# Head scaling and chunk work behind the convolution, decay rows behind exponentials, a later gate load, rotation in fewer operations

## The chip, the core and the metric

The kernel runs on one core of a Trainium2 chip. The metric is the device time of one execution in microseconds (us); smaller is better. The engines are TensorE (PE), VectorE (DVE), ScalarE (ACT), GpSimd (POOL) and SyncE (SP), which here only issues DMA transfers. Each engine runs its own instructions in the order in which they stand in its queue: an instruction that waits holds up all that stands behind it on that engine.

## What is computed

Two layers of a backbone over 512 latent tokens and 256 context tokens, in float32. Each layer normalises, projects once, and splits into three groups: a neighbourhood attention, a two-directional state-space mixer and a grouped-query attention. The lines that this change touches compute the following.

```
q = rms_norm(q.reshape(b, n, GQA_Q_HEADS, HEAD_DIM), q_norm_w)
k = rms_norm(k.reshape(b, n, GQA_KV_HEADS, HEAD_DIM), k_norm_w)
...
q = axial_rope(q, rows, cols)            # xh * cos + concat(-x2, x1) * sin
k = axial_rope(k, rows, cols)
...
xbc = jax.nn.silu(depthwise_conv(xbc, conv_w, conv_b))
...
seg = a_cum[:, :, :, None, :] - a_cum[:, :, None, :, :]
decay = jnp.exp(jnp.where(causal, seg, -jnp.inf))
g = jnp.einsum('bcthn,bcshn->bctsh', cr, br) * decay
y_diag = jnp.einsum('bctsh,bcshp->bcthp', g, xr)
...
y = y.reshape(zz.shape).astype(zz.dtype) * jax.nn.silu(zz)
```

Behind the mixers stand an output projection and a gated feed-forward block. The second layer (the last) gives results for the 512 latent tokens only.

## The kernel before

Float32 products on TensorE are made of pairs of a high and a low part, three matmuls each. A layer runs in stages. First come the projections of queries, keys and values; among them `p_kv` and `p_q`, which for each tile of 128 tokens take the raw grouped-query heads (one array of keys and two of queries, called here heads 0, 1 and 2) into `raws` (tile GR) and collect their sums of squares.

Then a loop runs over eight convolution blocks b. `p_xbc(b)` projects 128 channels over all tokens on TensorE (L348, into the PSUM tile S), VectorE clears the gap between context and latent tokens (memset L766), ScalarE takes the middle tap (L768), VectorE adds four taps (L773, four operations), ScalarE makes the tanh (L778) and VectorE finishes (L780, L782); one block later `p_xtr` transposes the result on TensorE (L796, six transposes in two halves), and ScalarE copies it out (L802). In the first layer, tiles of the gate z are projected between the blocks (L362), evacuated by ScalarE and VectorE (L814, L815) and written to DRAM (zsp). The loop also calls, for b below 3, `head_out(b)`: POOL multiplies the raw head by its norm weight, tile by tile (L680), and by the cosine (L686); VectorE makes the product with the sine in eight strided operations (L696, the rotation), adds (L697), and scales by the inverse root of the mean square (L699 for latent tokens, L701 for context tokens). `head_tr(b - 1)` transposes the head one block later (L708) and writes it to DRAM (gq). POOL meanwhile works through products for the next stage's modulation vectors (L239, 128x512 each), whose sums ScalarE takes (L240), and one power (L280) for the inverse roots of all heads, followed by the VectorE operations L282, L283 and L285.

Then 48 attention units (32 in the second layer) follow. Each makes scores on TensorE (L400, L403), a maximum on VectorE, the exponential on ScalarE (L420), the normalisation on POOL (L425), transposes (L434), their copies on ScalarE (L438) or VectorE (L440), and the product with the values (L446). Between units the list of events `ev` feeds in other work: `tick` advances the chunk work `diag` of the mixer by a step (two decay tiles wh and wl loaded from DRAM, crow, by SP; ScalarE's four decay-row additions L913; VectorE's L917, four; ScalarE's exponential L919; products on VectorE L924 to L933 and on POOL L928; matmuls L938 and L939), `steps` carries the chunk states, and `load_z`, the event at unit 6, has SP load z back into HZ (L1017).

What decides the order on each engine is a scheduler, which places the instructions by times that it simulates itself. `tc.issue_after(x)` is a constraint on it: what is traced in its block may not be placed ahead of instruction x on x's engine. It adds no wait, and it binds only the instructions of that one engine. The stages before the heads, the output projection and the feed-forward blocks are not touched by the change.

## Time and profile before

| | us |
|---|---|
| median of 3 runs | 1830.81 (1829.63 to 1834.84) |
| profiled execution | 1828.21 |
| its span | 1826.4 |
| TensorE busy | 1733.7 (95%) |
| VectorE, ScalarE, POOL busy | 1066.0, 682.7, 399.6 |
| mean granted TensorE clock | 0.976 |

The profiled execution lies 2.6 us under the median. In the 40 slices of the page the convolution blocks and the attention of the first layer lie at 150 to 450 us, those of the second at 1140 to 1400 us. A busy share is an average over stages: what a change to one stage is worth is read from the waits in that stage.

### The profile page before, as it was taken

To read this page: it belongs to the slowest core of one execution; us is meant where nothing else is said; L and a number is where in the kernel's file an instruction comes from. 1 tells how busy PE (TensorE), PEld (TensorE's weight loads), DVE (VectorE), ACT (ScalarE), POOL (GpSimd) and SP (SyncE) were. 2 spreads that over 40 slices of the span, in tenths; PEclk is the share of its full clock that TensorE was granted. 3 is DMA by queue.
4 is the path that set the end of the run, shared out by engine and by line. 5 is a ranking of instruction groups with operands and counts; after the bars stand their busy time and mean duration, and the time that the engine had idled before them with its cause. 6 is when DMAs were issued, how large, how long until landed. Compare 5 with 4: busy or idle time off the path is not lost.

```text
span 1826.4 us, 26611 instructions
## 1 busy us (share of the span) xinstructions
PE 1733.7 (95%) x10146; PEld 1475.2 (81%) x10146; DVE 1066.0 (58%) x2165; ACT 682.7 (37%) x1376; POOL 399.6 (22%) x429
## 2 busy tenths in 40 slices
PE   7998897899999999999999989998899999999998
PEld 3887785777878888888888878987777888888887
DVE  4659776886575455445554575576686743333334
ACT  4655664556253211121122234334555532222222
POOL 0398875643020000000000010421552100000000
PEclk9999998999989999999999999999899999999999
DMA  9643655422224343333344455233522333333332
GB/s 363 218 145 112 203 153 150 121 87 67 64 70 127 116 126 108 123 103 109 124 118 120 124 159 186 82 115 110 151 72 65 99 93 92 104 93 94 102 106 79
DMA packets 94319, 221.66 MB, mean 121 GB/s; under 512 B 18416, under 2 KB 26224, under 8 KB 94192
## 3 DMA queue, kind: packets, MB, share of 16 engines
q1 hardware_dynamic: 78096, 204.65, 36.6%
q10 hardware_dynamic: 16096, 15.31, 2.5%
q8 instruction: 80, 1.31, 0.3%
q14 instruction: 47, 0.39, 0.1%
HBM read 198.49 MB, written 21.43 MB: 120 GB/s over the span
## 4 chain that ended last, share of the span: by engine, by line
PE 77%; DVE 9%; DMA 6%; ACT 4%; issue 2%; POOL 2%; SPq 0%; ACTq 0%; DVEq 0%; POOLq 0%
PE S L348 60%; PE sm L446 3%; DMA wl<-crow 2%; PE PT L434 2%; PE PT L348 1%; PE PT L362 1%; PE sm L362 1%; DMA wr<-in_mod_wT_dram 1%; PE S L400 1%; PE sm L938 1%; PE sm L939 1%; PE PT L983 1%; DVE MB L773 1%; PE PT L996 1%; DVE wl L337 1%
## 5 line engine op out<-in xcount | busy, mean ns | idle before, releaser
L336 ACT ACTIVATE wh<-wr 128x1024 fp32r<-128x1024 f32 (+2 forms) x204 | 198.0, 972 | 723.8 <-PE S L348 550.7
L337 DVE TENSOR_TENSOR wl<-wr,wh 128x1024 fp32r<-128x1024 f32 (+2 forms) x204 | 231.2, 1134 | 178.9 <-ACT wh L336 177.0
L280 POOL TENSOR_TENSOR tiny<-tiny,mhalf 128x2 f32<-128x2 f32 (+2 forms) x17 | 28.7, 1689 | 1066.4 <-DVE tiny L1195 1018.7
L348 PE MATMUL S<-HY,wh 128*128 128x512 f32 (+1 forms) x716 | 215.8, 359 | 5.6 <-ACT HY L329 4.0
L348 PE MATMUL S<-HZ,wh 128*128 128x512 f32 (+1 forms) x716 | 213.4, 356 | 1.0 <-DVE HZ L330 1.0
L348 PE MATMUL S<-HS,wh 128*128 128x512 f32 (+1 forms) x716 | 213.0, 355 | 0.0
L348 PE MATMUL S<-HY,wl 128*128 128x512 f32 (+1 forms) x716 | 212.8, 355 | 0.1
L348 PE MATMUL S<-HS,wl 128*128 128x512 f32 (+1 forms) x716 | 209.7, 351 | 0.0
L242 DVE CUSTOM_DVE_ANT_0 PT<-wr,XFB 128x512 f32<-128x512 f32 x112 | 75.6, 716 | 185.6 <-DMA wr<-in_mod_wT_dram 185.5
L348 PEld LDWEIGHTS S<-HY,wh 128*128 128x128 f32 x716 | 118.6, 191 | 24.5 <-ACT HY L329 4.2
L348 PEld LDWEIGHTS S<-HZ,wh 128*128 128x128 f32 x716 | 119.5, 192 | 23.0 <-DVE HZ L330 2.8
L348 PEld LDWEIGHTS S<-HY,wl 128*128 128x128 f32 x716 | 118.8, 192 | 19.5 <-DVE wl L337 0.4
L348 PEld LDWEIGHTS S<-HS,wh 128*128 128x128 f32 x716 | 117.9, 190 | 18.2
L348 PEld LDWEIGHTS S<-HS,wl 128*128 128x128 f32 x716 | 116.6, 189 | 19.0
L348 PE MATMUL S<-PHA,wh 128*128 128x512 f32 (+1 forms) x358 | 105.8, 353 | 0.0
L348 PE MATMUL S<-PHB,wh 128*128 128x512 f32 (+1 forms) x358 | 104.5, 350 | 0.0
L348 PE MATMUL S<-GX,wh 128*128 128x512 f32 (+1 forms) x400 | 97.7, 350 | 0.4 <-DVE KA L1149 0.4
L425 POOL TENSOR_SCALAR pr<-pr,tiny 128x640 f32<-128x640 f32 (+2 forms) x80 | 67.8, 851 | 90.3 <-DVE tiny L424 66.1
L239 POOL TENSOR_TENSOR KA<-QN,XFB 128x512 f32<-128x512 f32 x48 | 68.5, 1430 | 40.8 <-ACT XFB L216 23.1
L434 PE MATMUL PT<-c,pr 128*128 128x128 f32 x384 | 65.0, 286 | 12.8 <-POOL pr L425 5.7
L1296 DVE TENSOR_TENSOR MB<-S,MA 128x768 f32<-128x768 f32 (+1 forms) x42 | 34.6, 823 | 70.7 <-PE S L348 70.7
L348 PEld LDWEIGHTS S<-GX,wh 128*128 128x128 f32 x400 | 65.9, 189 | 11.3 <-DVE KA L1149 0.8
(432 smaller groups left out, 3901.2 us busy)
## 6 DMA issues: line engine op xcount, KB each, us to landing
wr<-in_mod_wT_dram SPq DMA_DIRECT2D x56, 512.0 KB, 3.9
wr<-in_w_gate_dram SPq DMA_DIRECT2D x44, 512.0 KB, 3.6
wr<-in_w_up_dram SPq DMA_DIRECT2D x44, 512.0 KB, 3.6
wr<-in_w_blk_dram SPq DMA_DIRECT2D x28, 512.0 KB, 3.8
wr<-in_w_down_dram SPq DMA_DIRECT2D x32, 448.0 KB, 3.4
QN<-in_mod_wT_dram SPq DMA_DIRECT2D x48, 256.0 KB, 3.0
wr<-in_w_out_dram SPq DMA_DIRECT2D x32, 256.0 KB, 2.7
wr<-in_w_down_dram SPq DMA_DIRECT2D x16, 512.0 KB, 3.5
```

What stands on the lines that cost most here:

```text
L239: G.tensor_tensor(out=p_, in0=wv, in1=x, op=ALU.mult)
L242: V.tensor_tensor_reduce(out=p_, in0=wv, in1=x, scale=1.0, scalar=0.0, op0=ALU.mult, op1=ALU.add, accum_out=acc[:, o : o + 1],)
L280: POW.tensor_tensor(out=y, in0=v, in1=mhalf[:, 0:n], op=ALU.pow)
L336: S.activation(hi, raw, AF.Copy)
L337: V.tensor_tensor(lo, raw, hi.bitcast(F32), ALU.subtract)
L348: ins = PE.matmul(pt[:, c0:c1], lhsT=w, rhs=xx[:, c0:c1], start=(k == (0 if len(order) == 1 else order[0]) and i == 0), stop=(k == (nk - 1 ...
L362: PE.matmul(pt[:, 0:n], lhsT=s, rhs=w[:, o : o + n], start=(k == 0 and i == 0), stop=(k == KB - 1 and i == 2),)
L400: PE.matmul(st[:, o0:512], lhsT=Q[:, q0 : q0 + P], rhs=K[:, xk[0] : xk[1]], start=(i == 0), stop=(i == 1))
L425: G.tensor_scalar(out=p_, in0=p_, scalar1=m[:, 4:5], scalar2=1.0, op0=ALU.mult, op1=ALU.mult)
L434: PE.transpose(pt[:, k * P : (k + 1) * P], pr[j, qi][:, kk * P : (kk + 1) * P], ident)
L446: PE.matmul(pv[64 * j : 64 * j + 64, 0:P], lhsT=V2(kts[k], j), rhs=ph[j, qi][:, k, :], start=(k == 0), stop=(k == nkt - 1), tile_position= ...
L1296: V.tensor_tensor(gg[:, c0:c1], pu[:, c0:c1], sg[:, c0:c1], ALU.mult)
```

## The change

- `head_out(b)` is traced with `issue_after(conv_end[b])`, where conv_end[b] is the last VectorE operation of convolution block b. So VectorE's part of head b stands behind that block's finish. `head_tr` comes one block later (b = 2 to 4 in place of 1 to 3).
- `tick` is traced with `issue_after(conv_end[-1])`: all VectorE operations of the chunk work stand behind the finish of block 7.
- The four decay-row additions are traced with `issue_after(exps[-1])`: on ScalarE they stand behind the exponential that was traced last.
- `load_z` is the event at unit 14, not 6.
- In `head_out`, POOL's six (or four) 128x128 scalings become one of 128x768 (128x512), its four cosine products one of 128x512, and VectorE's eight rotation operations of 128x64 four of 128x128.

```diff
@@ -382,6 +382,8 @@
             r.append(K)
         return r
 
+    exps = []
+
     def attn(V2, xk, kts, qcols, bias, yout):
 
 
@@ -417,7 +419,7 @@
                 V.tensor_reduce(out=m[:, 0:1], in_=st[:, o0:768], op=ALU.max, axis=AX.X)
                 V.tensor_scalar_mul(m[:, 2:3], m[:, 0:1], -1.0)
             p_ = pr[j, qi] = T(sb, "pr", 3, [P, nk])
-            S.activation(p_, st[:, o0:768], AF.Exp, bias=m[:, 2:3], accum_out=m[:, 3:4])
+            exps.append(S.activation(p_, st[:, o0:768], AF.Exp, bias=m[:, 2:3], accum_out=m[:, 3:4]).ins)
 
@@ -674,26 +676,18 @@
             v4 = lambda ap: ap.rearrange("p t (h c) -> p t h c", c=64)
             v7 = lambda ap: ap.rearrange("p t (h f s c) -> p t h f s c", f=2, s=2, c=16)
             nt = n // P
-            for t in range(nt):
-                w3 = wvec.unsqueeze(1).to_broadcast([P, 2, 64])
-                rv = raw[:, t, :].rearrange("p (h c) -> p h c", c=64)
-                G.tensor_tensor(out=rv, in0=rv, in1=w3, op=ALU.mult)
+            w4 = wvec.unsqueeze(1).unsqueeze(1).to_broadcast([P, nt, 2, 64])
+            G.tensor_tensor(out=v4(raw[:, 0:nt, :]), in0=v4(raw[:, 0:nt, :]), in1=w4, op=ALU.mult)
             c = T(sb, "pr", 3, [P, 4, P])
             s = T(sb, "pr", 3, [P, 4, P])
-            for t in range(4):
-                rv = raw[:, t, :]
-                cb = cosT[:, t, :].unsqueeze(1).to_broadcast([P, 2, 64])
-                G.tensor_tensor(
-                    out=c[:, t, :].rearrange("p (h c) -> p h c", c=64), in0=rv.rearrange("p (h c) -> p h c", c=64),
-                    in1=cb, op=ALU.mult,
-                )
+            c4 = cosT.unsqueeze(2).to_broadcast([P, 4, 2, 64])
+            G.tensor_tensor(out=v4(c), in0=v4(raw[:, 0:4, :]), in1=c4, op=ALU.mult)
             sv = sinT.rearrange("p t (f s c) -> p t f s c", f=2, s=2)
-            for h in range(2):
-                x5 = raw[:, 0:4, 64 * h : 64 * h + 64].rearrange("p t (f s c) -> p t f s c", f=2, s=2)
-                o5 = s[:, :, 64 * h : 64 * h + 64].rearrange("p t (f s c) -> p t f s c", f=2, s=2)
-                for f in range(2):
-                    for k in range(2):
-                        V.tensor_tensor(o5[:, :, f, k, :], x5[:, :, f, 1 - k, :], sv[:, :, f, k, :], ALU.mult)
+            x6, o6 = v7(raw[:, 0:4, :]), v7(s)
+            for f in range(2):
+                for k in range(2):
+                    sb4 = sv[:, :, f, k, :].unsqueeze(2).to_broadcast([P, 4, 2, 16])
+                    V.tensor_tensor(o6[:, :, :, f, k, :], x6[:, :, :, f, 1 - k, :], sb4, ALU.mult)
             V.tensor_tensor(c, c, s, ALU.add)
             rb = r[:, 12 * i : 12 * i + 12].rearrange("p (t h) -> p t h", h=2).unsqueeze(3)
             V.tensor_tensor(v4(raw[:, 0:4, :]), v4(c), rb[:, 0:4].to_broadcast([P, 4, 2, 64]), ALU.mult)
@@ -754,6 +748,8 @@
 
         xs = [[slot("GX", F32, (P, 3, 256)) for _ in range(2)] for _ in range(2)]
         Bs, BT, CT, xb = [None] * 2, [None] * 2, [None] * 2, [None] * 8
+
+        conv_end = []
 
         def p_xbc(b):
             conly = last and b >= 6
@@ -777,9 +773,10 @@
             th = pt
             S.activation(th[:, 0:wid], ac[:, 0:wid], AF.Tanh)
             o = ac if b < 4 else slot("GT" if b < 6 else "GC")
-            V.scalar_tensor_tensor(o[:, 0:512], th[:, 0:512], 1.0, ac[:, 0:512], ALU.add, ALU.mult)
+            iv = V.scalar_tensor_tensor(o[:, 0:512], th[:, 0:512], 1.0, ac[:, 0:512], ALU.add, ALU.mult)
             if not conly:
-                V.scalar_tensor_tensor(o[:, 512:768], th[:, 516:772], 1.0, ac[:, 516:772], ALU.add, ALU.mult)
+                iv = V.scalar_tensor_tensor(o[:, 512:768], th[:, 516:772], 1.0, ac[:, 516:772], ALU.add, ALU.mult)
+            conv_end.append(iv.ins)
             if b >= 4:
                 (BT, CT)[b // 6][b % 2] = o
             xb[b] = o
@@ -882,9 +879,10 @@
             if b:
                 p_xtr(b - 1)
             if b < 3:
-                head_out(b, qnw[l] if b else knw[l], r, ntok if b else NT)
-            if 1 <= b < 4:
-                head_tr(b - 1, ntok if b > 1 else NT)
+                with tc.issue_after(conv_end[b]):
+                    head_out(b, qnw[l] if b else knw[l], r, ntok if b else NT)
+            if 2 <= b < 5:
+                head_tr(b - 2, ntok if b > 2 else NT)
 
         def hb(ap, w):
             return ap.unsqueeze(2).to_broadcast([P, ap.shape[1], w])
@@ -908,9 +906,10 @@
                 d_ = nc.sync.dma_start(t.rearrange("p h t -> p (h t)"), crow[i][:, o : o + 512].to_broadcast([P, 512]))
             rows_in.append(d_.ins)
             yield
-            for h in range(4):
-                o = 8 + h0 + h
-                S.activation(Wb[:, h, :], Wb[:, h, :], AF.Identity, bias=ncum[:, c, o : o + 1])
+            with tc.issue_after(exps[-1]):
+                for h in range(4):
+                    o = 8 + h0 + h
+                    S.activation(Wb[:, h, :], Wb[:, h, :], AF.Identity, bias=ncum[:, c, o : o + 1])
             yield
             for h in range(4):
                 o = h0 + h
@@ -1089,6 +1088,10 @@
         st_ = steps()
 
         def tick(t):
+            with tc.issue_after(conv_end[-1]):
+                tick_(t)
+
+        def tick_(t):
             if t % 3 == 1 and t // 3 + 1 < nd:
                 next(dgs[t // 3 + 1])
             for k in range(t // 3, t // 3 - 2, -1):
@@ -1100,7 +1103,7 @@
         ev += [(u, 1, lambda: next(st_, None)) for u in spread_over(36, U[2], U[3])]
         if not last:
             ev.append((U[4], 2, lambda: gate(4, 5)))
-        ev.append((6, 2, load_z))
+        ev.append((14, 2, load_z))
         ev.append((U[5], 2, lambda: gate(1, 2)))
         ev.append((U[6], 2, lambda: gate(0, 3)))
         ev.append((3 * nu / 4, 2, lambda: y_in(1)))
```

How the scheduler's order changes, at three places.

VectorE in the first layer, at the finish of convolution block 0. GR_1206 is head 0, GR_1207 and GR_1208 are heads 1 and 2; MB is the convolution's result and S its PSUM tile; tiny_37x are the inverse roots. Before:

```order
L282 SCALAR_TENSOR_TENSOR tiny_372_1748<-tiny_371_1746 128x36
L283 TENSOR_TENSOR tiny_372_1748<-tiny_372_1748,tiny_370_1744 128x36
L285 SCALAR_TENSOR_TENSOR tiny_373_1751<-tiny_372_1748,tiny_371_1746 128x36
L659 MEMSET tiny_1873_10643 128x36
L699 TENSOR_TENSOR GR_1206<-pr_1853,tiny_373_1751 128x512
L701 TENSOR_TENSOR GR_1206<-GR_1206,tiny_373_1751 128x256
L701 TENSOR_TENSOR GR_1207<-GR_1207,tiny_373_1751 128x256
L701 TENSOR_TENSOR GR_1208<-GR_1208,tiny_373_1751 128x256
L780 SCALAR_TENSOR_TENSOR MB_1809<-S_1759,MB_1809 128x512
L782 SCALAR_TENSOR_TENSOR MB_1809<-S_1759,MB_1809 128x256
L697 TENSOR_TENSOR pr_2009<-pr_2009,pr_2010 128x512
L766 MEMSET S_1876 128x4
```

The same place now:

```order
L282 SCALAR_TENSOR_TENSOR tiny_372_1748<-tiny_371_1746 128x36
L283 TENSOR_TENSOR tiny_372_1748<-tiny_372_1748,tiny_370_1744 128x36
L776 SCALAR_TENSOR_TENSOR MB_1809<-S_1759,MB_1809 128x512
L778 SCALAR_TENSOR_TENSOR MB_1809<-S_1759,MB_1809 128x256
L690 TENSOR_TENSOR pr_1849<-GR_1206,c_214 128x8x16
L285 SCALAR_TENSOR_TENSOR tiny_373_1751<-tiny_372_1748,tiny_371_1746 128x36
L690 TENSOR_TENSOR pr_1849<-GR_1206,c_214 128x8x16 x3
L661 MEMSET tiny_1873_10607 128x36
L695 TENSOR_TENSOR GR_1206<-GR_1206,tiny_373_1751 128x256
L691 TENSOR_TENSOR pr_1848<-pr_1848,pr_1849 128x512
L693 TENSOR_TENSOR GR_1206<-pr_1848,tiny_373_1751 128x512
L762 MEMSET S_1864 128x4
```

The finish of the block (L780 and L782, now L776 and L778) has moved ahead of the head's scalings; the rotation of head 0 (now L690), which stood in the stage before, has moved in between it and the memset of block 1 (L766, now L762).

VectorE in the first layer, convolution block 5; zt is the gate's tile. Before:

```order
L766 MEMSET S_2517 128x4
L815 SCALAR_TENSOR_TENSOR zt_2602<-zt_2602,sm_2577 128x256
L773 SCALAR_TENSOR_TENSOR MB_2567<-S_2517,c_214,MB_2567 128x770
L773 SCALAR_TENSOR_TENSOR MB_2567<-S_2517,c_214,MB_2567 128x771
L815 SCALAR_TENSOR_TENSOR zt_2631<-zt_2631,PT_2606 128x256
L917 SCALAR_TENSOR_TENSOR wh_2847<-wh_2847,dtr_2486,wl_2848 128x128 x2
L773 SCALAR_TENSOR_TENSOR MB_2567<-S_2517,c_214,MB_2567 128x771
L917 SCALAR_TENSOR_TENSOR wh_2847<-wh_2847,dtr_2486,wl_2848 128x128 x2
L773 SCALAR_TENSOR_TENSOR MB_2567<-S_2517,c_214,MB_2567 128x770
L780 SCALAR_TENSOR_TENSOR GT_2574<-S_2517,MB_2567 128x512
L782 SCALAR_TENSOR_TENSOR GT_2574<-S_2517,MB_2567 128x256
```

The same place now:

```order
L762 MEMSET S_2481 128x4
L769 SCALAR_TENSOR_TENSOR MB_2531<-S_2481,c_214,MB_2531 128x770
L812 SCALAR_TENSOR_TENSOR zt_2566<-zt_2566,sm_2541 128x256
L769 SCALAR_TENSOR_TENSOR MB_2531<-S_2481,c_214,MB_2531 128x771
L812 SCALAR_TENSOR_TENSOR zt_2595<-zt_2595,PT_2570 128x256
L769 SCALAR_TENSOR_TENSOR MB_2531<-S_2481,c_214,MB_2531 128x771
L769 SCALAR_TENSOR_TENSOR MB_2531<-S_2481,c_214,MB_2531 128x770
L776 SCALAR_TENSOR_TENSOR GT_2538<-S_2481,MB_2531 128x512
L778 SCALAR_TENSOR_TENSOR GT_2538<-S_2481,MB_2531 128x256
```

The four L917 of the first chunk are gone from between the taps; they stand behind block 7.

ScalarE in the second layer, at the first attention units; wl is a decay tile, pr an attention tile, PHA and PHB copies of transposed ones. Before:

```order
L913 ACTIVATE wl_12061<-wl_12061,dtr_11504 128x128 x4
L913 ACTIVATE wl_12186<-wl_12186,dtr_11504 128x128 x4
L438 ACTIVATE PHA_12050<-PT_12051 128x384
L438 ACTIVATE PHA_12050<-PT_12056 128x256
L420 ACTIVATE pr_12016,tiny_12012<-S_12007,tiny_12012 128x640
L919 ACTIVATE wh_12060<-wh_12060 128x512
L989 ACTIVATE HS_12071<-PT_12068 128x512
L919 ACTIVATE wh_12185<-wh_12185 128x512
L420 ACTIVATE pr_12046,tiny_12042<-S_12037,tiny_12042 128x640
L438 ACTIVATE PHB_12090<-PT_12091 128x384
L420 ACTIVATE pr_12082,tiny_12078<-S_12073,tiny_12078 128x640
```

The same engine and units now:

```order
L422 ACTIVATE pr_11948,tiny_11944<-S_11939,tiny_11944 128x640
L440 ACTIVATE PHA_11982<-PT_11983 128x384
L422 ACTIVATE pr_11978,tiny_11974<-S_11969,tiny_11974 128x640
L440 ACTIVATE PHA_11982<-PT_11988 128x256
L912 ACTIVATE wl_11630<-wl_11630,dtr_11423 128x128 x4
L988 ACTIVATE HS_12003<-PT_12000 128x512
L422 ACTIVATE pr_12014,tiny_12010<-S_12005,tiny_12010 128x640
L440 ACTIVATE PHB_12022<-PT_12023 128x384
L918 ACTIVATE wh_11629<-wh_11629 128x512
L440 ACTIVATE PHB_12052<-PT_12053 128x384
L422 ACTIVATE pr_12045,tiny_12041<-S_12036,tiny_12041 128x640
L440 ACTIVATE PHB_12052<-PT_12058 128x256
```

The decay rows (L913, now L912) of two chunks stood ahead of two copies and an exponential; now the first chunk's stand behind the fourth exponential, and the next chunk's follow further on.

## Rows read from the trace of the kernel before

**Rows 1.** The page's head and its busy time of the engines.
```profile
span 1826.4 us, 26611 instructions
PE 1733.7 (95%) x10146; PEld 1475.2 (81%) x10146; DVE 1066.0 (58%) x2165; ACT 682.7 (37%) x1376; POOL 399.6 (22%) x429
```

**Rows 2.** Busy us of five engines per stretch, granted clock (PEclk), DMA share, GB/s.
```profile
150.00:200.00 50.00, 39.97 (x250) 36.03 (x250) 42.51 (x65) 25.28 (x67) 39.99 (x31) 0.89 0.39 127
200.00:250.00 50.00, 47.44 (x307) 42.76 (x306) 37.79 (x43) 36.53 (x91) 48.99 (x37) 0.97 0.62 203
250.00:300.00 50.00, 35.99 (x223) 30.84 (x222) 34.71 (x78) 24.35 (x60) 26.38 (x32) 0.86 0.49 137
1250.00:1300.00 50.00, 40.64 (x290) 36.24 (x290) 30.56 (x85) 22.03 (x56) 20.53 (x26) 0.88 0.54 161
1300.00:1350.00 50.00, 46.51 (x328) 36.88 (x328) 37.72 (x103) 24.85 (x63) 29.05 (x37) 0.91 0.37 95
```

**Rows 3.** TensorE's waits, 150 to 275 us: in total, times, longest.
```profile
PE PT L796 <- DVE zt L815: 7.3, 2, 4.9
PE PT L796 <- DVE MB L780: 5.1, 1, 5.1
PE PT L796 <- DVE GT L780: 2.0, 2, 1.5
```

**Rows 4.** VectorE's timeline, 150 to 206 us: start, duration, engine, line, tiles.
```profile
153.62 1.23 DVE L696 TENSOR_TENSOR pr<-GR,c 128x64 f32<-128x64 f32 x8
165.24 1.69 DVE L699 TENSOR_TENSOR GR<-pr,tiny 128x512 f32<-128x512 f32 x1
166.85 3.21 DVE L701 TENSOR_TENSOR GR<-GR,tiny 128x256 f32<-128x256 f32 x3
169.99 0.68 DVE L780 SCALAR_TENSOR_TENSOR MB<-S,MB 128x512 f32<-128x512 f32 x1
171.63 0.69 DVE L699 TENSOR_TENSOR GR<-pr,tiny 128x512 f32<-128x512 f32 x1
177.04 0.41 DVE L815 SCALAR_TENSOR_TENSOR zt<-zt,PT 128x256 f32<-128x256 f32 x1
185.63 7.37 DVE L696 TENSOR_TENSOR pr<-GR,c 128x64 f32<-128x64 f32 x8 [2.98 <-DMA gq<-pr]
```

**Rows 5.** TensorE's timeline at the second half of convolution 0's transposes.
```profile
177.50 0.55 PE L796 MATMUL PT<-c,MB 128*128 128x128 f32 x3
```

**Rows 6.** POOL's timeline, 148 to 180 us: the power and one modulation product.
```profile
152.63 7.06 POOL L280 TENSOR_TENSOR tiny<-tiny,mhalf 128x36 f32<-128x36 f32 x1 [0.37 <-DVE tiny L275]
173.38 1.29 POOL L239 TENSOR_TENSOR KA<-QN,XFB 128x512 f32<-128x512 f32 x1 [3.93 <-ACT KA L240]
```

**Rows 7.** Durations by line over the program: min/median/max ns, first and last start.
```profile
L917 DVE SCALAR_TENSOR_TENSOR wh<-wh,dtr,wl x80: 333/348/8287, 244.2 to 1354.6; 128x128 f32<-128x128 f32 x80
L773 DVE SCALAR_TENSOR_TENSOR MB<-S,c,MB x64: 741/1018/1023, 157.9 to 1253.9; 128x770 f32<-128x770 f32 x28, 128x771 f32<-128x771 f32 x28, 128x510 f32<-128x510 f32 x4, 128x511 f32<-128x511 f32 x4
```

**Rows 8.** ScalarE's waits at the decay rows: 150:345, then 1262:1345.
```profile
ACT wl L913 <- DMA wl<-crow: 13.2, 7, 5.3
...
ACT wl L913 <- DMA wl<-crow: 14.7, 6, 3.6
```

**Rows 9.** TensorE's waits, 275 to 345 us.
```profile
PE S L400 <- ACT pr L420: 4.4, 1, 4.4
PE sm L446 <- DMA GR<-in_rpb_dram: 1.9, 1, 1.9
```

**Rows 10.** TensorE's waits, 1262 to 1345 us.
```profile
PE PT L983 <- ACT PHA L438: 5.9, 1, 5.9
PE PT L434 <- ACT PHA L438: 2.3, 1, 2.3
PE PT L983 <- ACT PHB L438: 1.9, 1, 1.9
```

**Rows 11.** Transfers issued from 262 to 300 us: count, KB each, us to landing.
```profile
HZ<-zsp SPq DMA_DIRECT2D x4, 384.0 KB, 6.2
```

## The prediction

> **What bounds the kernel now.** I read the busy times first, then the stretches, then who ends TensorE's waits. TensorE is busy 1733.7 us of a span of 1826.4 [rows 1], so all its idle time together is 93 us, and no change that leaves the matmuls as they are can win more than that and what the slow clock costs. The change touches three stretches, so only their idle time counts [rows 2]: in the first layer's convolution blocks TensorE does 39.97 of 50 us from 150 on and 47.44 in the next 50; at the seam to the attention 35.99 of 50; in the second layer's attention 40.64 and 46.51. VectorE and POOL are each about 40 of 50 us busy in the first of them. The granted clock falls there too, to 0.86 to 0.91: of its two levels, 2.4 and 1.2 GHz, the lower holds for some 14 us of 250 to 300 (2 x 0.14 x 50), 12 of 1250 to 1300 and 9 of 1300 to 1350. TensorE had been waiting ahead of each of these. Work under the lower level takes at most twice as long, so half of those times is the most that the clock can give back.
>
> The waits name their places. In the convolution blocks TensorE waits at the transposes for VectorE: 5.1 us for the finish of block 0, 7.3 in two pieces for the gate's evacuation, 2.0 for later finishes [rows 3]. At the seam it waits 4.4 us for an exponential [rows 9], in the second layer 5.9, 2.3 and 1.9 for ScalarE's copies [rows 10]. Behind both stands one cause: ScalarE's decay rows sit at the head of its queue waiting for crow transfers, 13.2 us in the first layer and 14.7 in the second [rows 8], and exponentials and copies wait behind them.
>
> **Convolution blocks 0 to 2 (head work moved).** Block 0's finish ran at 169.99 because 1.69 + 3.21 us of head scalings stood ahead of it [rows 4]. In the new order it stands ahead, so the wait of 5.1 us goes. What is late next is the second half of the same transposes: it began at 177.50 [rows 5], just as the gate's evacuation at 177.04 had freed its PSUM tile [rows 4], and that evacuation now stands behind the whole of head 0. So the gain is not 5.1 us: VectorE's list decides. Before, heads cost it, between 162 and 195 us: 1.69 and twice 0.69 (the scalings), 3.21 (the context's), twice 0.69 (the sums, of the size of the short scaling), 7.37 (a rotation), and 2.98 of waiting for the transfer that frees the rotation's tile [rows 4]: 18.0 us. Now each of three heads brings four rotation operations, a context scaling, a sum and a scaling. Undisturbed that is 4 x 0.35 (L917 has the size, [rows 7]) + 0.41 (the evacuation at 177.04 has it) + 0.69 + 0.69 = 3.2 us. At the pace that POOL's work allows it is 4 x 0.92 (7.37 / 8) + 1.07 + 1.69 + 1.69 = 8.1 us. Three heads: 9.6 to 24.3, against 18.0, so from -8.4 to +6.3 us. POOL is busy four fifths of the stretch, which puts a head at 0.8 x 8.1 + 0.2 x 3.2 = 7.1 us. Two heads fall where VectorE is full, 14.2 against 18.0, or -3.8; the third falls behind 200 us, where VectorE has 12 of 50 us free [rows 2], and costs little. Since each new head now delays a memset and an evacuation which had run before it, I book half: **-2 us**. Merging the operations is already in these figures; POOL's saved operations free time on an engine nobody waits for here. The transposes of heads, one block later, feed loads of much later units: nothing.
>
> The same pace has a rule. Beside POOL's 7.06 us power the eight rotations of 153.62 took 1.23 us in all [rows 4, 6]; beside its products of 1.29 us one L917 took 8.29 us, as long as six of them [rows 6, 7]; the taps, which read PSUM, kept to 1.02 us throughout [rows 7]. The Trainium skill (SBUF — State Buffer, "Who interferes with whom") says that a VectorE operation with two SBUF inputs and a GpSimd operation that reads SBUF exclude each other for one whole instruction, PSUM readers not. The taps agree, the power and the 8.29 us do not: one was no obstacle, the other far more than one instruction. By the rule a rotation operation would cost at most 1.29 + 0.35 = 1.64 us, a head 11.0, two heads 22, and this term +4 in place of -2.
>
> **Blocks 4 to 7 (chunk work behind the last block).** Two L917 took 8.29 us and more between the taps of block 5. They leave this queue. The waits of 2.0 us [rows 3] and of 7.3 - 4.9 = 2.4 for the gate at 264 go, since taps and evacuation then follow without it: **-4.4 us**, between 0 and -6 with the clock. The moved work, three chunks' L917 at 12 x 0.35 us and products of about as much again, some 8 us, comes to the attention, where VectorE is busy 34.7 of 50 [rows 2]. The bounds are 0 and +8; there is room for most: **+3 us**. The gates that read the chunks' results are events of units 22, 46 and 47 of 48, which leaves the chunks time.
>
> **Seam and decay rows, first layer.** With the rows behind exponentials the 4.4 us wait loses its cause. The 1.9 us for the bias transfer [rows 9] loses one too: the four gate loads of 384 KB, 6.2 us each to land [rows 11], stood ahead of it on SP and now come eight units later. What is next is POOL's normalisation and VectorE's maximum, so I take three quarters of 6.3, 4.7, and a fifth of the 7 us of clock: **-6 us** (from 0 to -13). Edge to watch: the rows are then later by two exponentials, and so is each chunk.
>
> **Second layer.** The term is the decay rows alone. The three waits are 10.1 us [rows 10]; three quarters, 7.6, and 3 of at most 10.5 us of clock: **-11 us** (from -2, where the transfers stay what is late, to -20).
>
> **Sum.** -2 - 4.4 + 3 - 6 - 11 = -20.4 us. Against the profiled execution of 1828.2 that is 1807.8; it lay 2.6 under the median, so 1810.
>
> **Rivals.** (1) The order holds but the next wait takes its place: a crow transfer still ends late, and exponentials then wait for maxima, copies for transposes. For it: ScalarE is idle half the time in these stretches [rows 2], so its order may only pass the wait on. Against it: TensorE's large waits end on ScalarE within a microsecond of the decay rows. Then the second layer gives -3, the seam -1, the blocks -4, the moved work +3: -5, so 1826. (2) All the waits and their clock go: -8.4 - 6 - 13 - 20 + 0 = -47, so 1784; against it speaks that POOL and VectorE are nearly full in the blocks. (3) Slower: one rotation operation per head is starved as the L917 was, 8.29 us, now in front of the memset of the next block, for which ScalarE, the evacuation and the transposes wait. Three heads add 25 us to the sum of -20.4: +4.6, with the chunk's delay at its +8 bound +9.6, so 1840. It decides from 20 us on, that is from more than two such operations. For it: the rotations leave a stretch where POOL ran the power and enter one in which it runs products back to back. Against it: POOL stops there when ScalarE is held up, once for 3.93 us [rows 6], which lets VectorE through, and the eight rotations of 185.63, in the thick of it, took 7.37 together.
>
> **How the numbers follow.** The forecast has a chance of 0.57, rival 1 0.20, rival 2 0.12, rival 3 0.11. The range goes from the forecast's better half towards rival 2, 1795, to just beyond rival 1, 1831; outside lie half of rival 2, rival 3 and a little of the forecast's edge. A measurement of this kernel can tell about 0.3%, 5.5 us. Rival 1 lies at that edge, three quarters within it: faster 0.57 + 0.12 + 0.05 = 0.74, same 0.15, slower 0.11.
>
> **What would show it.** In the changed kernel: block 0's finish near 164 us and no 5 us wait ahead of its transposes, but a new wait of up to 10 us ahead of their second half; no L917 among taps and none of 8 us; the wait of ScalarE at decay rows for crow under 5 us in each layer; TensorE 44 us busy or more in 1250 to 1300. I am wrong if the waits at decay rows shrink and TensorE's do not (rival 1), if rotation operations take over 2 us each (rival 3), or if TensorE is late at the end of the convolution blocks by more than 5 us.

## The result, and the profile after

The changed kernel takes 1806.85 us (1798.04 to 1810.22) against 1830.22 us for the kernel before, measured beside it: a ratio of 0.9865, with a 95% interval from 0.9827 to 0.9902. The forecast was 1810 us, faster. The sum came out; two of its five terms did not, as the stages show. All medians here leave out one slow execution, of 3370 us, of the kernel called e10 below.

The page of the changed kernel begins as follows (compare [rows 1]).

```profile
span 1806.9 us, 26557 instructions
PE 1727.2 (96%) x10146; PEld 1472.2 (81%) x10146; DVE 1072.8 (59%) x2141; ACT 682.5 (38%) x1376; POOL 395.0 (22%) x385
```

The stretches of [rows 2] in the changed kernel, with the same columns (the busy times of TensorE, its weight loads, VectorE, ScalarE and POOL, then the granted clock, the DMA share and GB/s):

```profile
150.00:200.00 50.00, 39.07 (x243) 35.03 (x242) 45.76 (x51) 23.29 (x61) 40.68 (x25) 0.90 0.31 96
200.00:250.00 50.00, 40.76 (x268) 37.30 (x269) 38.72 (x50) 34.67 (x84) 44.50 (x34) 0.90 0.63 204
250.00:300.00 50.00, 45.56 (x297) 39.85 (x296) 32.15 (x81) 25.22 (x63) 32.28 (x37) 0.90 0.46 136
1250.00:1300.00 50.00, 44.23 (x336) 36.93 (x336) 37.67 (x111) 27.48 (x71) 31.49 (x39) 0.97 0.57 160
1300.00:1350.00 50.00, 46.73 (x358) 37.20 (x353) 42.90 (x99) 28.41 (x71) 30.55 (x38) 1.00 0.40 113
```

TensorE does less than before in the convolution blocks (40.76 in place of 47.44 from 200 on) and more in both attentions. Fixed windows mix two stages when one has shifted, so for all that follows I took three marks from TensorE's timeline: the first scores of the first layer (the end of its convolution blocks), and for each layer the stretch from its first scores to its last product with the values. In us, from the one profiled execution of each kernel:

| kernel | first scores at | attention, first layer | attention, second layer | median |
|---|---|---|---|---|
| before | 270.4 | 177.9 | 148.1 | 1830.2 |
| changed | 273.1 | 164.8 | 137.0 | 1806.9 |
| difference | +2.6 | -13.1 | -11.1 | -23.4 |

The rest differs by 1.7 us between the two attentions and 0.4 behind the second, both longer. So the whole gain lies in the two attentions, and the convolution blocks lost time.

**The blocks.** TensorE's waits from 150 to 275 us in the changed kernel (in total, times, longest; compare [rows 3]). L793 are the transposes, L799 ScalarE's copy of them, L812 the gate's evacuation, L841 a matmul for the decays:

```profile
PE PT L793 <- ACT GX L799: 9.1, 2, 8.8
PE sm L841 <- DVE zt L812: 6.4, 1, 6.4
PE PT L793 <- DVE pr L294: 2.6, 1, 2.6
PE PT L793 <- DVE MB L776: 2.0, 1, 2.0
```

The wait for block 0's finish fell from 5.1 to 2.0 us, and one of 8.8 us came behind it. The timelines tell why (start, duration, line; compare [rows 4]). VectorE first, then POOL, then ScalarE:

```profile
152.62 1.35 DVE L275 TENSOR_SCALAR tiny<-tiny 128x36 f32<-128x36 f32 x1
165.11 1.28 DVE L282 SCALAR_TENSOR_TENSOR tiny<-tiny 128x36 f32<-128x36 f32 x1 [1.72 <-POOL tiny L280]
167.53 0.68 DVE L776 SCALAR_TENSOR_TENSOR MB<-S,MB 128x512 f32<-128x512 f32 x1
170.08 4.00 DVE L690 TENSOR_TENSOR pr<-GR,c 128x128 f32<-128x128 f32 x3
176.82 0.06 DVE L762 MEMSET S<- 128x4 f32 x1
184.61 5.35 DVE L690 TENSOR_TENSOR pr<-GR,c 128x128 f32<-128x128 f32 x4
202.40 4.65 DVE L690 TENSOR_TENSOR pr<-GR,c 128x128 f32<-128x128 f32 x4
213.12 0.06 DVE L762 MEMSET S<- 128x4 f32 x1
218.22 0.41 DVE L812 SCALAR_TENSOR_TENSOR zt<-zt,sm 128x256 f32<-128x256 f32 x1
```

```profile
151.07 4.68 POOL L680 TENSOR_TENSOR GR<-GR,c 128x768 f32<-128x768 f32 x2
155.68 2.33 POOL L239 TENSOR_TENSOR KA<-QN,XFB 128x512 f32<-128x512 f32 x1
157.95 7.12 POOL L280 TENSOR_TENSOR tiny<-tiny,mhalf 128x36 f32<-128x36 f32 x1
```

```profile
176.92 0.99 ACT L764 ACTIVATE MB<-S,c 128x772 f32<-128x772 f32 x1 [7.36 <-DVE S L762]
180.75 0.63 ACT L240 ACTIVATE KA<-KA 128x512 f32<-128x512 f32 x1 [1.35 <-DVE zt L812]
181.64 0.48 ACT L799 ACTIVATE GX<-PT 128x384 f32<-128x384 f32 x1
```

Head 0's rotation and scalings stand between block 0's finish at 167.53 and block 1's memset at 176.82. ScalarE's middle tap waits 7.36 us for that memset; the copy L799 stands on ScalarE behind the tap, and behind a wait of 1.35 us for the gate's evacuation, which is late on VectorE too; and TensorE's next transposes wait for the PSUM tile that the copy frees. Head 2 (from 202.40 to 210.5) does much the same to the memset of 213.12 and to the evacuation of 218.22, which the decay matmul waits for; a modulation product (L250) and a weight conversion (L337) stand in between there. And the finish itself was late: the two merged scalings of heads 1 and 2 need the last token tile, so 4.68 us of POOL stand in a piece, with a modulation product of 2.33 us behind them, ahead of the power. It began at 157.95, 4.0 us after its input (L275) was there, in place of 152.63 [rows 6].

Two more marks show what that cost: TensorE's transposes of block 0 (their first half) and of block 3 (their second half). From the one to the other it is 57.5 us before and 68.5 in the changed kernel; from the second to the first scores, 42.2 before and 36.3 changed. So the blocks with heads lost 11.0 us behind a start that was 2.4 us earlier, and blocks 4 to 7 won 5.9.

**The attentions.** ScalarE's wait at the decay rows for crow, 13.2 and 14.7 us before [rows 8], does not occur in the changed kernel in either stretch. (Counted from 1235 us on, as below, the second figure is 15.7.) In the second layer TensorE's waits from 1235 to 1345 us begin with these (compare [rows 10]); of those for ScalarE's copies none over 0.6 us is left:

```profile
PE PT L436 <- POOL pr L427: 3.9, 4, 2.1
PE sm L448 <- DVE tiny L420: 1.2, 1, 1.2
```

At the seam of the first layer the 4.4 us of [rows 9] are not gone but passed on (TensorE's timeline):

```profile
281.62 0.69 PE L402 MATMUL S<-KA,QN 128*128 128x384 f32 x1 [3.71 <-ACT pr L422]
```

The exponential that it waits for stands on ScalarE behind the tanh of block 7, which waits for that block's taps. Eight of the experiments below show the same 3.71 us.

### The profile page after: what moved, and what is told of

It is laid out like the page before. It is cut to its first block, busy times and chain, and to the rows that moved or that the text cites. A ratio compares the mean times of both kernels' runs of the same rounds, so it can differ in the third digit from the quotient of the medians.

```text
span 1806.9 us, 26557 instructions
## 1 busy us (share of the span) xinstructions
PE 1727.2 (96%) x10146; PEld 1472.2 (81%) x10146; DVE 1072.8 (59%) x2141; ACT 682.5 (38%) x1376; POOL 395.0 (22%) x385
## 4 chain that ended last, share of the span: by engine, by line
PE 77%; DVE 11%; POOL 3%; DMA 3%; issue 3%; ACT 2%; ACTq 0%; SPq 0%; DVEq 0%; POOLq 0%
PE S L348 61%; PE sm L448 2%; PE PT L362 2%; PE PT L436 2%; PE PT L348 1%; PE sm L362 1%; DMA wr<-in_mod_wT_dram 1%; PE S L402 1%; POOL tiny L280 1%; DVE wh L916 1%; DVE pr L690 1%; PE S L405 1%; DVE wl L337 1%; POOL KA L239 1%; PE S L189 1%
## 5 line engine op out<-in xcount | busy, mean ns | idle before, releaser
L337 DVE TENSOR_TENSOR wl<-wr,wh 128x1024 fp32r<-128x1024 f32 (+2 forms) x204 | 233.7, 1147 | 179.3 <-ACT wh L336 177.0
L427 POOL TENSOR_SCALAR pr<-pr,tiny 128x640 f32<-128x640 f32 (+2 forms) x80 | 73.5, 922 | 67.6 <-DVE tiny L426 56.1
L436 PE MATMUL PT<-c,pr 128*128 128x128 f32 x384 | 65.6, 285 | 11.1 <-POOL pr L427 5.2
```

Of the source, the lines that this page charges most:

```text
L337: V.tensor_tensor(lo, raw, hi.bitcast(F32), ALU.subtract)
L427: G.tensor_scalar(out=p_, in0=p_, scalar1=m[:, 4:5], scalar2=1.0, op0=ALU.mult, op1=ALU.mult)
L436: PE.transpose(pt[:, k * P : (k + 1) * P], pr[j, qi][:, kk * P : (kk + 1) * P], ident)
```

## The experiments

Each is named by what it changes. An execution's time scatters by 0.3 to 0.6% either way; part of it is TensorE's pace in the feed-forward blocks, which no kernel here changes (last section). So effects of a few us are read from the stages of the one profiled execution of each kernel, and the medians are given beside them.

| kernel | first scores at | attention, first layer | attention, second layer | median | ratio to before (95%) |
|---|---|---|---|---|---|
| changed, without heads' part (e1) | 268.0 | 162.6 | 138.6 | 1800.5 | 0.9844 (0.9818 to 0.9870) |
| changed, without chunk part (e2) | 276.2 | 170.9 | 137.7 | 1811.6 | 0.9912 (0.9881 to 0.9943) |
| changed, without rows' part (e3) | 274.4 | 179.5 | 143.2 | 1833.1 | 1.0025 (1.0002 to 1.0048) |
| changed, without gate's part (e4) | 272.5 | 163.8 | 138.0 | 1806.2 | 0.9875 (0.9838 to 0.9912) |
| before, with rows' part (e5) | 276.7 | 171.2 | 135.7 | 1808.6 | 0.9889 (0.9857 to 0.9921) |
| changed, without merging (e6) | 272.1 | 164.1 | 138.2 | 1798.5 | 0.9837 (0.9807 to 0.9867) |
| changed, POOL's products left out (e7) | 257.7 | 163.9 | 135.3 | 1790.8 | one look |
| e1, scalings behind the power (e8) | 272.9 | 163.1 | 137.8 | 1806.0 | 0.9882 (0.9848 to 0.9916) |
| before, with rows' and chunk part (e9) | 263.5 | 164.6 | 136.0 | 1801.4 | 0.9851 (0.9828 to 0.9874) |
| e9, rotation on POOL (e10) | 268.2 | 167.3 | 139.7 | 1800.2 | 0.9840 (0.9819 to 0.9860) |
| e10, with heads' part (e11) | 272.8 | 164.6 | 135.5 | 1801.8 | 0.9849 (0.9830 to 0.9869) |
| before, with chunk part (e12) | 267.1 | 176.3 | 145.8 | 1827.2 | 1.0002 (0.9975 to 1.0029) |

The attentions fall into groups. In the first layer the nine kernels with the rows' and the chunk part lie at 162.6 to 167.3 us, the two with the rows' part only (e2, e5) at 170.9 and 171.2, the three without the rows' part (before, e3, e12) at 176.3 to 179.5. In the second layer all with the rows' part lie at 135.3 to 139.7, those without it at 143.2 to 148.1.

**One part taken out of the changed kernel at a time.** The heads' part:

```diff
-                with tc.issue_after(conv_end[b]):
-                    head_out(b, qnw[l] if b else knw[l], r, ntok if b else NT)
-            if 2 <= b < 5:
-                head_tr(b - 2, ntok if b > 2 else NT)
+                head_out(b, qnw[l] if b else knw[l], r, ntok if b else NT)
+            if 1 <= b < 4:
+                head_tr(b - 1, ntok if b > 1 else NT)
```

> The changed kernel without the first part: the heads' VectorE work and transposes are traced as before, the other four parts stay. Theory A (from the trace of the changed kernel: the new waits of 8.8 us and 6.5 us at the transposes of blocks 0 to 3 come from the rotations standing ahead of the next memset): the first scores of layer one start at 265 to 271 us in place of 273, no wait over 6 us there, and the time is 2 to 8 us under the changed kernel's 1807. Theory B (the prediction's term: queueing the heads behind the finish wins some 2 us of 18 of head work): first scores at 273 to 277 us, time 1808 to 1812.

First scores came 5.1 us earlier (268.0), the largest waits from block 0's transposes on were 3.6 and 2.9 us in place of 8.8 and 6.4, and the median is 6.4 us lower. Theory A: the heads' new place costs time. The two ratios' intervals overlap, so the size rests on the stage. There it is more than 5.1: e1 lost 5.8 us to a late conversion of weights (L337) ahead of block 0's transposes. From block 0's to block 3's transposes it takes 58.8 us, the changed kernel 68.5. Of the other kernels with the rotation on VectorE and POOL's products beside it, those with merged heads behind the finish (e2, e3, e4) take 68.2 to 69.1 there, e6, which has them unmerged, 65.2, and those with the heads in their old place (before, e8, e9, e12) 56.6 to 58.6, apart from e5 (63.6), with a stall told in the last section. One reason shows in e1's timeline: two heads are rotated ahead of block 0's transposes, at 137.92 and 158.05, in 0.89 and 0.95 us for all four operations (the second beside POOL's power); behind the finish the first two heads took 4.48 and 5.35.

```profile
137.92 0.89 DVE L690 TENSOR_TENSOR pr<-GR,c 128x128 f32<-128x128 f32 x4
158.05 0.95 DVE L690 TENSOR_TENSOR pr<-GR,c 128x128 f32<-128x128 f32 x4
```

The chunk part:

```diff
         def tick(t):
-            with tc.issue_after(conv_end[-1]):
-                tick_(t)
-
-        def tick_(t):
```

> The changed kernel without the second part: VectorE's chunk work may again be placed among the convolution blocks. Theory A (the prediction's terms, -4.4 us in blocks 4 to 7 and +3 in the attention): about 1.5 us slower than the changed kernel, 1807 to 1810. Theory B (the 13 us that the first layer's attention won come from the chunk work's new place): 8 to 13 us slower, 1815 to 1820, the loss between the first scores and the last values of layer one. If decay rows behind exponentials already hold the chunks back, nothing: within 2 us and almost the same order.

The median is 4.7 us higher, short of theory B's 8, and the intervals of the two ratios overlap. By the stages it is 9.3 us to the last values of the first layer, 6.1 of them in the attention: theory B's place and size. The profiled execution as a whole shows nothing of it (1807.9 us); in it TensorE was faster in the untouched feed-forward blocks. Theory A's +3 us for the moved work is not borne out. But theory B's reason does not hold either. Without the chunk part VectorE's chunk work is still not in the blocks, as the expectation's last case supposed, because its decay additions (L916 here) need the rows. In e2 only two mask products stand ahead of block 7's finish (L776):

```profile
280.09 0.29 DVE L923 TENSOR_TENSOR SA<-sm,c 128x128 f32<-128x128 f32 x1
280.30 0.28 DVE L924 TENSOR_TENSOR SB<-sm,c 128x128 f32<-128x128 f32 x1
284.25 0.69 DVE L776 SCALAR_TENSOR_TENSOR GC<-S,MB 128x512 f32<-128x512 f32 x1 [0.36 <-ACT S L774]
291.44 1.81 DVE L916 SCALAR_TENSOR_TENSOR wh<-wh,dtr,wl 128x128 f32<-128x128 f32 x3
```

From block 3's transposes to the first scores e2 takes the same 36.3 us as the changed kernel. What made its attention longer is the order that the scheduler chose further on.

The rows' part:

```diff
-            with tc.issue_after(exps[-1]):
-                for h in range(4):
+            for h in range(4):
...
```

> The changed kernel without the third part: decay rows may again be placed ahead of exponentials. Theory A (the prediction's: the rows at the head of ScalarE's queue are the cause of the waits at the seam and in layer two, 6 and 11 us): 12 to 18 us slower, 1819 to 1825, and layer two's stretch from first scores to last values back from 137 to about 148 us. Theory B (the later gate load, not the order of the rows, cleared the crow transfers): under 4 us slower, that stretch stays under 140 us.

The whole gain went, and a little more: 26 us over the changed kernel. The first layer's attention is back at 179.5 us, the second's went halfway, to 143.2. Theory A in kind, and more than its 12 to 18 us: the other four parts without this one do not help.

The gate's load:

```diff
-        ev.append((14, 2, load_z))
+        ev.append((6, 2, load_z))
```

> The changed kernel with the gate's load back at unit 6. Theory A (the prediction's: worth the 1.9 us wait for the bias transfer and no more): 0 to 3 us slower, 1806 to 1810. Theory B (the four 384 KB loads ahead of the crow loads on SP are what held up the decay rows): 8 us slower or more, most of it in layer two's attention, with waits of ScalarE at decay rows of over 8 us there.

Nothing, in the median and within about 1 us in each stage. Theory A, at its lower end.

The merging (all of the fifth part undone):

```diff
-            w4 = wvec.unsqueeze(1).unsqueeze(1).to_broadcast([P, nt, 2, 64])
-            G.tensor_tensor(out=v4(raw[:, 0:nt, :]), in0=v4(raw[:, 0:nt, :]), in1=w4, op=ALU.mult)
+            for t in range(nt):
+                w3 = wvec.unsqueeze(1).to_broadcast([P, 2, 64])
+                rv = raw[:, t, :].rearrange("p (h c) -> p h c", c=64)
+                G.tensor_tensor(out=rv, in0=rv, in1=w3, op=ALU.mult)
...
```

> The changed kernel without the fifth part: POOL's scalings and products and VectorE's rotations in the small operations of before. Theory A (each operation waits for about one of POOL's, so their number counts): the rotation of heads 1 and 2 takes 7 to 9 us in place of 5, first scores of layer one at 275 to 281 us in place of 273, time 2 to 8 us over the changed kernel's 1807. Theory B (what the merging wins there it loses by making the power, and with it the finish of block 0, late): the power starts at 152 to 154 us in place of 158, the wait at block 0's first transposes goes, first scores within 2 us of 273, time within 3 us of 1807.

First scores at 272.1, within 1 us of the changed kernel: theory B. The power began at 151.45 and block 0's finish stood at 163.61 in place of 167.53, while the rotations took 5.85, 4.05 and 6.24 us (eight operations each) against 4.48, 5.35 and 4.65 (four each). Half the operations save about half a microsecond a head. The median, 8 us lower, fell outside what B allowed (3 us), at the edge of the scatter.

**Parts put alone on the kernel before.** The rows:

> The kernel before with the third part alone: decay rows behind exponentials. Theory A (the prediction's: the rows at the head of ScalarE's queue are the cause of the waits at the seam and in layer two): 15 to 25 us faster than before, 1803 to 1813; of that 6 to 12 us in the first layer's attention and 6 to 11 in the second's. Theory B (the parts need each other: rows behind exponentials help only once VectorE's chunk work is out of the convolution blocks): under 6 us faster, 1822 or more.

The edit is the reverse of e3's. The time is 19 us lower: theory A, 12.4 us of it in the second layer's attention, a little over its 6 to 11, and 6.7 in the first's. The blocks were 6 us late for another reason, told in the last section.

The chunk part alone, the reverse of e2's edit:

> The kernel before with the second part alone: VectorE's chunk work behind block 7, decay rows wherever the scheduler puts them. Theory A (the gains of the two parts add, -19 for the rows alone and -27 for both): 6 to 10 us faster than before, 1819 to 1823, first scores of layer one at 262 to 267 us. Theory B (while the decay rows stand ahead of exponentials, moving only VectorE's half of the chunk work leaves ScalarE waiting as long, and later): within 5 us of before, 1824 to 1834, with 10 us or more of ScalarE's waits for crow in each layer.

Nothing: theory B. First scores came 3.4 us earlier, but the attentions stayed long. ScalarE's wait at the decay rows in the second layer, 1235 to 1345 us (L918 there), and TensorE's longest behind it, are about those of before (15.7 and 5.9):

```profile
ACT wl L918 <- DMA wl<-crow: 15.2, 7, 3.6
```

```profile
PE PT L988 <- ACT PHA L440: 6.2, 1, 6.2
```

Both together:

> The kernel before with the second and third parts alone: chunk work behind block 7, decay rows behind exponentials. Theory A (these two make the whole gain; heads and merging cost some 5 us in the first layer's blocks, the gate's load nothing): 1796 to 1802, first scores of layer one at 265 to 271 us, that layer's attention 162 to 166 us, the second's 135 to 139. Theory B (merging carries part of it, together with either place of the heads): 1804 to 1812, first scores at 272 or later.

1801.4 us, theory A: two of the five parts make the whole gain. First scores, at 263.5, came even before its 265 to 271. The blocks end 9.6 us before those of the changed kernel, with the waits of before in them (5.1 and 4.3 us; compare [rows 3]):

```profile
PE PT L801 <- DVE MB L784: 5.1, 1, 5.1
PE PT L801 <- DVE zt L820: 4.3, 1, 4.3
```

No kernel here is shown by its times to beat the changed one, since the intervals overlap; e6, e10, e1, e9 and e11 are the lowest of those that compute the whole, at 1798.5 to 1801.8 us.

**Why the heads' work is slow.** POOL's products left out:

```diff
-                        G.tensor_tensor(out=p_, in0=wv, in1=x, op=ALU.mult)
-                        S.activation(p_, p_, AF.Copy, accum_out=acc[:, o : o + 1])
+                        S.activation(p_, wv, AF.Copy, accum_out=acc[:, o : o + 1])
```

> The changed kernel with POOL's products for the modulation vectors left out: ScalarE sums the raw weights, so the modulation of later stages is another, while every transfer and all other work stays. One look. Theory A (VectorE's head work is slow because POOL works beside it): rotation operations of 0.3 to 0.5 us each in place of 1.2 to 1.3, a head's work 3 to 4 us in place of 7 to 10, the waits of 8.8 and 6.5 us at the transposes under 4 each, first scores of layer one at 256 to 266 us in place of 273. Theory B (the operations are slow by themselves, by their strides): they stay above 1 us and first scores at 270 or later.

Theory A, and more: a head's work took 2.7 us, under its 3 to 4. The rotation operation (L689 here: min/median/max ns over the program):

```profile
L689 DVE TENSOR_TENSOR pr<-GR,c x24: 280/284/288, 172.5 to 1188.0; 128x128 f32<-128x128 f32 x24
```

TensorE's only wait over half a microsecond between 150 and 265 us is one of 0.9, and first scores came at 257.7, 15.4 us earlier. With POOL's products beside it the same operation takes 1.2 to 1.3 us on average (4.00 for three, 5.35 and 4.65 for four). The 15.4 us are not the heads' alone: the edit also relieves all other VectorE work with two SBUF inputs, and ScalarE no longer waits for a product (up to 2.06 us in the changed kernel).

**Two attempts to use that.** Behind the power (the scalings of heads 1 and 2 in e1's kernel, traced with an order-only edge on the power):

> The changed kernel without the first part (as in the first experiment, 1800) and with POOL's scalings of the heads kept behind the power of the inverse roots. Theory A (the merged scalings ahead of the power made block 0's finish late): the power starts at 152 to 154 us in place of 158, block 0's first transposes at 165 to 168 in place of 172, first scores of layer one 2 to 5 us earlier than that kernel's 268, time 1796 to 1799. Theory B (the gate's evacuation decides, and the later scalings make heads 1 and 2 late): first scores at 267 to 272, time 1799 to 1804.

This did not test what it was to test: VectorE was itself late with the power's input, so the power began no earlier (158.72), and block 0's transposes waited 7.2 us. Theory A's condition was not met; the time is no lower than e1's.

The rotation on POOL, without and with the heads' part (e10, e11):

```diff
-                        V.tensor_tensor(o5[:, :, f, k, :], x5[:, :, f, 1 - k, :], sv[:, :, f, k, :], ALU.mult)
+                    G.tensor_tensor(out=o6[:, :, :, f, k, :], in0=x6[:, :, :, f, 1 - k, :], in1=sb4, op=ALU.mult)
...
```

> The kernel of e9 with the rotation (four operations a head) on POOL in place of VectorE, so that it shares no port with POOL's products. Theory A (VectorE's contended head work in the convolution blocks is what TensorE waits for): the stall of 7 us at 185 us on VectorE goes, first scores 3 to 8 us earlier than in e9, time 3 to 8 us less. Theory B (POOL, 80 to 98% busy there, hands the time on through the modulation sums on ScalarE, or the head's scalings wait for POOL): first scores within 2 us of e9 or later.

> The kernel of e10 with the first part as well: the heads' sums and scalings behind the finish of their block. Theory A (queueing the heads behind the finish was right, and only the rotations made it late): the wait at block 0's first transposes under 1 us, the one at their second half under 5, first scores 255 to 264 us, time 1789 to 1797 and under e10. Theory B (any head work ahead of the next memset costs what it saved): first scores within 2 us of e10, time the same.

Theory B for e10: first scores 4.7 us later than in e9, the time the same. For e11 neither: the time is again the same, but first scores came 4.6 us after e10's, past theory B's 2 us. The rotation's 5 to 7 us left VectorE, and in their place one single addition of the two products waited (e10's VectorE timeline):

```profile
193.29 11.87 DVE L698 TENSOR_TENSOR pr<-pr,pr 128x512 f32<-128x512 f32 x1 [0.63 <-POOL pr L697]
```

In e11 the same operation took 12.45 us. TensorE waited 5.7 and 6.1 us for what stands behind it on VectorE.

## Why the prediction was right, and where it was not

**The decay rows in the second layer: right.** -11 us was forecast; -11.1 came, -12.4 with the rows alone (e5), -2.3 and -4.9 without them (e12, e3). The cause is shown: in every kernel whose rows stand behind exponentials ScalarE does not wait for crow in these stretches, where they don't it waits 10.5 to 15.7 us in this layer (e3, e12, before).

**Seam and rows in the first layer: right in size, not in place.** -6 us was forecast, and the rows alone give -6.7 over that attention (e5). But the 4.4 us wait was passed on to the next exponential as 3.71; the gain is that more work runs ahead of it: the third unit's scores come 8.6 us after the first's, in place of 14.9. The gate's load, which was to clear the bias transfer, does nothing (e4): that wait of 1.9 us is gone in all twelve experiments too, also in those with the load at unit 6 (e4, e5, e9 to e12).

**Blocks 0 to 2: wrong.** The step that failed is the booking of -2 us: block 3's transposes came 8.5 us later than before. Of the bracket only the upper end was near: heads cost VectorE 7.3, 10.3 and 8.2 us, 25.8 in all, against 18.0 before, or +7.8, somewhat beyond the +6.3 that POOL's pace gave. I took 7.1 a head, and then let the third count for little because VectorE has slack behind 200 us. It has, but head 2 stands in front of one memset and one evacuation there, and TensorE waited 6.4 us for that: the share of a stretch that an engine is free says nothing of an operation that is queued behind the wrong one. The wait of up to 10 us that the text looked for came, 8.8; it was read as part of a balance that would still be negative. e1 shows that the heads' place costs 5.1 us in all, and 9.7 between the transposes of block 0 and block 3. The merging was said to be in these figures, and its cost was not: the late power, with block 0's finish at 167.53 where the text looked for 164 (it came at 163.61 without the merging, e6).

The rule of the Trainium skill (SBUF — State Buffer, "Who interferes with whom") gave +4 for this term, by the prediction's estimate. It was nearer than my -2, and e7 and the 1.3 us of a rotation operation agree with it: about one POOL product per operation.

**Blocks 4 to 7: right.** -4.4 us was forecast; from block 3's transposes to the first scores it is 5.9 us less in the changed kernel, 6.5 less with the chunk part alone (e12) and 6.7 in e9. The heads' loss hides it in the changed kernel's first scores. Not foreseen was that the rows' part does the same by itself (e2: 5.9 less).

**The moved chunk work: not borne out.** +3 us was forecast for VectorE's 8 us more in the attention. That was too large from the start: of the three chunks' twelve L917 only four stood ahead of the first scores before (244.25 to 254.25), the other eight were in the attention already. Taking the part out makes that attention 6.1 us longer (e2), and adding it to the rows makes it 6.6 us shorter (e9 against e5). Moved work is not what these two pairs measure: in e5, as in e2, only the two mask products stand ahead of block 7's finish, and the first decay addition comes at 291.67. Only e12 moves the work by this part, and there that attention is 1.6 us shorter than before, with the decay rows still ahead of exponentials. Why the pairs differ isn't settled. TensorE's waits of 0.4 us and more in that attention add up to 10.6 in e9 and 15.0 in e5, and from 260 to 450 us its granted clock was 0.90, 1.00, 1.00 and 1.00 in e9's four windows, 0.93, 0.97, 0.93 and 1.00 in e5's, but no run tells which step of the order does it.

So that the sum of -20.4 met -19.5 between the profiled executions is in part luck, since two errors cancelled: the blocks, forecast at -6.4, gave +2.6, and the first layer's attention, forecast at -3, gave -13.1. What carried the forecast was the reading of ScalarE's queue.

## What to carry to other kernels

Look at the head of each in-order queue: a small operation that waits for a transfer there costs whatever stands behind it, and an order-only edge behind the work that others wait for was worth more here than the saved operations (19 us in e5, against a median 8 us lower without the merging in e6). Such an edge has two sides: before queueing work behind X, list what stands behind that work on the same engine and who waits for it. And a merged operation starts when its last input is there, so a merge on one engine can delay the next operation by more than it saves.

## What the runs showed that was not expected

A VectorE operation with two SBUF inputs can wait for as long as POOL runs back to back, not for one operation: 8.29 us for the L917 of [rows 7], 11.87 and 12.45 us in e10 and e11 (ten operations of POOL in a row in e10; the addition ended where they did), 6.93 and 8.06 us for two conversions of weights (L337) in e5, which made its blocks late, 7.61 in e6 and 7.96 in e2. Undisturbed, the addition takes 0.69 us. A single rotation operation is hit as well, as the prediction's rival 3 feared, though not in the changed kernel: 6.97 us in e12's blocks, 7.60 ahead of the blocks in e5 and e9. Which operation is hit changes with any shift of the order; the changed kernel has none over 3 us from 150 to 280 us. This adds several us of scatter between orders in the blocks; e1 and the changed kernel are alike in this from 150 us on, which makes their comparison between the transposes the safest there. Its neighbours often get through after one POOL operation; what decides between the two isn't shown.

TensorE's pace differed between the profiled executions at the same granted clock. From 600 to 700 us, in a stretch without a wait, the changed kernel did 567 matmuls and e2's kernel 579:

```profile
600.00:700.00 100.00, 100.00 (x567) 86.66 (x567) 52.87 (x117) 17.17 (x18) 0.00 (x0) 1.00 0.41 121
```

```profile
600.00:700.00 100.00, 100.00 (x579) 88.19 (x578) 54.80 (x125) 18.24 (x19) 0.00 (x0) 1.00 0.39 122
```

e8's execution ran at e2's pace there, the others at the changed kernel's. Between the two attentions e2's execution was 11.9 us shorter than the changed kernel's, which is why stages, not totals, had to separate the parts.
